# The prompt's up-projection by seven products of half blocks, with the weight sums on POOL

## The chip, the cores and the metric

One NeuronCore of a Trainium2 chip runs the whole kernel; one launch, all inputs and outputs in HBM. The metric is the time of that core on the device in microseconds. Engines: PE (TensorE, with PEld for its weight loads), DVE (VectorE), ACT (ScalarE), POOL (GpSimd) and SP, which issues most of the DMAs.

## The reference, cut to what matters

An encoder layer is run on two sequences, "prompt" (512 tokens) and "sample" (1024 tokens), with the same weights in float32. After a mixer the layer has a channel sub-layer, and its first product is the widest of the layer: 1024 channels to 2 x 2816.

```python
D_MODEL, D_FF, CONV_F_WIDTH = 1024, 2816, 3
h = rms_norm(x, g_pre_ffn) * (1.0 + sc2) + sh2
up = depthwise_conv(h @ w_up, ffn_conv_w, ffn_conv_b, CONV_F_LEFT)   # 3 taps along the tokens
val, gate = up[..., :D_FF], up[..., D_FF:]
f = (jax.nn.gelu(gate) * val) @ w_down
x = x + gt2 * rms_norm(f, g_post_ffn)
```

`mod = silu(c) @ w_ada + b_ada` gives the scales, shifts and gates (`sc2`, `sh2`, `gt2`) for each sequence.

## The kernel before

Activations stand channel-major: 128 channels on the partitions, tokens along the free axis. Every float32 operand of a product is split into a high part (a rounded copy, on ACT, type fp32r) and a low part (the rest, a subtraction on DVE); a product is three passes, high x high, high x low and low x high, added up in PSUM. Each matmul brings its own weight load of 128x128.

The program is a flat list of `Step`s. A step has matmuls (`mm`), what follows them (`post`, evictions and elementwise work), and often a `Unit`, a block of 128 x 1024 weights: `load_unit` brings it by a DMA of SP into one of three `raw` buffers, `prep_unit` splits it into one of four `hl` buffers. `emit` (L192) writes the steps in order; ahead of step i it prepares the weights of the steps up to i + 3 (`AHEAD`) and has the loads go three units ahead (`RAW_BUFS`); `defer(fn, d)` puts a piece of work d steps later. There is no other scheduler: each engine runs its instructions in the order in which this loop wrote them, waits for the semaphores of others, and lets nothing overtake.

The prompt's up-projection is `up_steps` (L1391). It makes 22 pairs of column tiles (gate, then value), 44 steps of 8 channel blocks x 3 passes = 24 matmuls, each 128 weights wide with all 512 tokens moving. `conv_f` (L1371) evicts a tile from PSUM: ACT scales the centre tap, DVE adds the two others (`scalar_tensor_tensor`, 128x511). The gate goes through gelu on ACT, DVE multiplies, and the result `fo` stays in SBUF for the down-projection. Into this list `weave` puts the 24 side steps of `ada_steps(5)` and `gate_steps`: 16 dot products of 128x1024 on DVE (L360) that form the gate `gt2`, four small DVE instructions on them (the last two write `gtg`), a PE transpose of `gtg` (`gate_rows`, L390), and a DMA round trip; one side step stands ahead of each product step from the third on.

Before it run the sample's output projection, after it the prompt's down-projection (`rows_steps`), and later the sample's up-projection `up_quads` (L1213). That one already makes two column tiles (20 pairs of 22) by seven products of blocks rather than eight: halves of the 1024 channels and halves of the 1024 tokens, so that a product moves 512 tokens; all block sums there are done by DVE, the parts of a product are split 512 columns at a time (`part`, L1289 and L1290).

Of the kernel before, what the change touches and what calls it, by code (L numbers as in the profile page):

```python
# [45 lines left out]
V_FW = 168  # L46
V_FB = 300
# [4 lines left out]
class Seq:  # L52
    def __init__(self, name, idx, n, x, y):
        self.name, self.idx, self.n, self.x, self.y = name, idx, n, x, y
        self.nf = 1024 // n
        self.tt = n // 128
        self.chunks = n // 512
        self.groups = KT // self.nf
        self.pq_tiles = self.tt // 2
# [7 lines left out]


class Step:
    def __init__(self, mm=None, post=None, unit=None, pre=None, loads=()):  # L70
        self.mm, self.post, self.unit, self.pre, self.loads = mm, post, unit, pre, loads


class Enc:
# [104 lines left out]
    def prep_to(self, k):  # L179
        while self.pp < min(len(self.units), k):  # L180
            self.load_to(self.pp + 1)
            u = self.units[self.pp]
            if u.unit is not None and (u.unit.parts or u.unit.dma) and self.pp + 2 > k:
                break
            if u.pre is not None:
                u.pre()
            if u.unit is not None and u.unit.whole:
                self.prep_unit(u.unit)
            self.pp += 1
            self.load_to(self.pp + RAW_BUFS)  # L190

    def emit(self):  # L192
        pos = 0
        for i, s in enumerate(self.steps):
            while self.rl < min(len(self.steps), i + LOAD_AHEAD + 1):
                for f in self.steps[self.rl].loads:
                    f()
                self.rl += 1
            self.load_to(self.pp + RAW_BUFS)
            self.prep_to(pos + AHEAD + 1)  # L200
            if s.unit is not None or s.pre is not None:
                pos += 1
            if s.mm is not None:
                s.mm()
            if s.post is not None:
                s.post()
            due = [f for t, f in self.late if t <= self.now]
            self.late = [(t, f) for t, f in self.late if t > self.now]
            for f in due:
                f()  # L210
            self.now += 1
# [960 lines left out]
    def quad_sums(self, hb):  # L1172
# [37 lines left out]
            steps += [Step(post=both), Step(post=parts(("t1", "t2", "t3", "t4")))]  # L1210
        return steps

    def up_quads(self, sq, hb, dst, plain):  # L1213

        nc = self.nc
        steps = []
        table = self.a["w_up"]
# [32 lines left out]
        for g in range(plain):  # L1250
            box = {}
# [20 lines left out]
            for m, post in ((FT + g, post_g), (g, post_v)):  # L1272
                u = Unit(table[m], KT * 128, on_act=True)
                steps.append(Step(mm=lambda u=u, mm_all=mm_all: mm_all(u, 0), unit=u, post=post))

        ring = {"n": 0}
        quads = []
        for g in range(plain, FT):
            ua, ub = (Unit(table[m], KT * 128, whole=False) for m in (FT + g, g))
            b, w = {}, {}  # L1280
# [52 lines left out]
            def post(i, b=b, g=g):  # L1333
                def f():
# [21 lines left out]
            plan = [((0, 0), "p", 0), ("t2", "p", 1), ("t1", "q", 0), ("t3", "q", 1), ((1, 0), "p", 0), ((1, 1), "q", 0),  # L1356
                    ("t4", "q", 1)]
# [30 lines left out]
                    in1=acc[:, f, o], op0=ALU.mult, op1=ALU.add)  # L1388
        return acc

    def up_steps(self, sq, hb, fo):  # L1391
        nc = self.nc
        steps = []
        xh, xl = (lambda: hb["hi"]), (lambda: hb["lo"])
        for g in range(FT // sq.nf):
            box = {}

            def post_g(ps, g=g, box=box):
                acc = self.conv_f(sq, ps, FT + g * sq.nf)
                nc.scalar.activation(out=acc, in_=acc, func=AF.Gelu_apprx_tanh)  # L1400
                box["g"] = acc

            def post_v(ps, g=g, box=box):
                acc = self.conv_f(sq, ps, g * sq.nf)
                nc.vector.tensor_tensor(out=acc, in0=acc, in1=box.pop("g"), op=ALU.mult)
                fo[g] = acc
            steps += self.fm_steps(sq, self.a["w_up"], range(FT + g * sq.nf, FT + (g + 1) * sq.nf), xh, xl, post_g,
                                   on_act=True)
            steps += self.fm_steps(sq, self.a["w_up"], range(g * sq.nf, (g + 1) * sq.nf), xh, xl, post_v,
                                   on_act=True)  # L1410
        steps[-1].post, last = None, steps[-1].post

        def done():
            last()
            hb.clear()
        steps[-1].post = done
        return steps


def weave(main, side, at, stride):  # L1420
    out = []
    side = list(side)
    for i, s in enumerate(main):
        if i >= at and (i - at) % stride == 0 and side:
            out.append(side.pop(0))
        out.append(s)
    return out + side


# [12 lines left out]
@with_exitstack
def encoder(ctx: ExitStack, tc: tile.TileContext, a, outs):
    nc = tc.nc
    e = Enc(ctx, tc, a, outs)
    p, s = e.p, e.s
    x2 = {q.name: e.dram([q.n, D], "x2" + q.name) for q in (p, s)}
    sig = {q.name: {(w, g): e.dram([128, 1024], f"sg{q.name}{w}{g}") for w in range(2) for g in range(q.groups)}
           for q in (p, s)}
    with tc.manual_schedule():  # L1450
        e.setup()
        h1 = {"p": {}, "s": {}}
        h2 = {"p": {}, "s": {}}
        hs = {q: {} for q in "ps"}
        yb = {q: {} for q in "ps"}
        pq = {q: {} for q in "ps"}
        z = {q: {} for q in "ps"}
        mg = {q: {} for q in "ps"}
        gate = {(q, i): {} for q in "ps" for i in range(2)}
        fo = {q: {} for q in "ps"}  # L1460

        def mix(q, heads):
            at = 4
            out = heads[:at] + e.pq_steps(q, pq[q.name], heads[:at]) + heads[at:]
            out += e.ya_steps(q, h1[q.name], hs[q.name], yb[q.name])
# [12 lines left out]
        _, heads = e.mix_heads(s, h1["s"], hs["s"], sig["s"])
        steps += place(mix(s, heads), e.ada_steps(3) + e.ada_steps(2, (1,)) + e.ada_steps(4),
                       [0, *range(8, 37), *range(36, 46), *range(40, 48)])  # L1480
        pa, pbt = e.h_steps(p, x2["p"], 1, h2["p"])
        steps += weave(e.merge_steps(s, yb["s"], z["s"], sig["s"], mg["s"]),
                       e.gate_steps(s, 0, gate["s", 0]) + pa, 8, 1)
        steps += weave(e.rows_steps(s, a["w_o"], mg["s"], gate["s", 0], a["x_sample"], x2["s"]), pbt, 4, 2)

        steps += weave(e.up_steps(p, h2["p"], fo["p"]),
                       e.ada_steps(5) + [Step()] * 2 + e.gate_steps(p, 1, gate["p", 1]), 2, 1)
        sa, sbt = e.h_steps(s, x2["s"], 1, h2["s"], quads=True)
        steps += weave(e.rows_steps(p, a["w_down"], fo["p"], gate["p", 1], x2["p"], outs[0]),
                       sa + sbt, 0, 1)  # L1490
        fs = e.dram([FT, 128, 1024], "fs")
        steps += place(e.up_quads(s, h2["s"], fs, 2), e.quad_sums(h2["s"]), [0, 0, 1, 1, 2, 2, 3, 3])
        steps += weave(e.rows_steps(s, a["w_down"], fo["s"], gate["s", 1], x2["s"], outs[1], last=True, fsrc=fs),
                       e.gate_steps(s, 1, gate["s", 1]), 4, 1)

        e.begin(steps)
        e.lead_in(p, a["x_prompt"], first, h1["p"], (2, 2, 2, 2))
        e.emit()
        e.flush()
# [118 lines left out]
```

## Time and profile before

| | us |
|---|---|
| median of 3 runs (lowest, highest) | 2091.42 (2090.84, 2091.93) |
| the profiled execution, its own time | 2091.33 |
| its span, first to last instruction | 2089.6 |
| PE busy, of the span | 2063.0 |
| DVE busy | 1411.0 |
| ACT busy | 948.0 |
| POOL busy | 69.9 |

The span leaves 1.7 us around it. A matmul's row shows a duration that overlaps with the next one's, so what a matmul costs is read from the distance between starts, not from its duration. The same holds to a lesser degree for DVE: a row lasts a little longer than the distance to the next start.

### The profile page before, as it was taken

How to read it: one execution, taken by the hardware profiler on the slowest of the kernel's cores; microseconds unless marked ns; L12 is line 12 of the kernel's file. 1: busy time of each engine (PE TensorE's matmuls, PEld its weight loads, DVE VectorE, ACT ScalarE, POOL GpSimd, SP SyncE). 2: the span in 40 equal slices, each digit the busy share in tenths (PEclk: the TensorE clock that was granted, in tenths of full speed). 3: DMA queues.
4: the chain of work that ended last, by engine and by line, in shares of the span. 5: the costliest groups of instructions: out<-in, count | busy, mean ns of one | idle time of the engine just before them, and what ended most of it. 6: DMA issues, size and time to landing. Idle time of an engine off the chain costs nothing.

```text
span 2089.6 us, 24382 instructions
## 1 busy us (share of the span) xinstructions
PE 2063.0 (99%) x9591; PEld 1685.7 (81%) x9591; DVE 1411.0 (68%) x1805; ACT 948.0 (45%) x1224; POOL 69.9 (3%) x154
## 2 busy tenths in 40 slices
PE   7999999999999999999999999999999999999998
PEld 6877788888888888888888888887888888888886
DVE  5667788667677556666576555759788888875543
ACT  2387555264654722145333336533444444444442
POOL 0100010100000000000100001000000000000000
PEclk9999999999999999999999999999999999999999
DMA  9933666643333325434543324232122222384322
GB/s 338 315 120 135 221 240 202 211 141 107 100 116 107 106 88 210 166 101 162 193 150 111 98 104 171 91 115 78 70 85 77 81 91 71 105 317 172 132 98 104
DMA packets 94451, 297.76 MB, mean 143 GB/s; under 512 B 9312, under 2 KB 20992, under 8 KB 93824
## 3 DMA queue, kind: packets, MB, share of 16 engines
q1 hardware_dynamic: 87968, 278.24, 37.9%
q0 software_dynamic: 5216, 13.74, 2.2%
q10 hardware_dynamic: 1152, 4.23, 0.5%
q8 instruction: 75, 1.23, 0.2%
q14 instruction: 40, 0.33, 0.0%
HBM read 248.93 MB, written 47.24 MB: 142 GB/s over the span
## 4 chain that ended last, share of the span: by engine, by line
PE 89%; DVE 5%; ACT 3%; issue 2%; DMA 1%; POOL 0%; DVEq 0%; POOLq 0%; SPq 0%; ACTq 0%
PE ps L223 88%; PE ps L226 1%; ACT th L733 1%; ACT th L723 1%; ACT ea L731 1%; DVE cf L1386 0%; DVE hx L113 0%; DVE hq L1184 0%; DVE th L754 0%; DVE th L759 0%; DVE th L757 0%; DVE hl L113 0%; ACT hl L110 0%; ACT xn L450 0%; ACT th L735 0%
## 5 line engine op out<-in xcount | busy, mean ns | idle before, releaser
L223 PE MATMUL ps<-hh,hl 128*128 128x512 f32 x2144 | 632.5, 394 | 3.7 <-DVE hl L113 2.9
L223 PEld LDWEIGHTS ps<-hh,hl 128*128 128x128 f32 x2144 | 402.2, 188 | 99.8 <-DVE hl L113 4.1
L223 PE MATMUL ps<-hl,ah 128*128 128x512 f32 x1440 | 452.8, 395 | 0.0
L113 DVE TENSOR_TENSOR hl<-raw,hl 128x1024 fp32r<-128x1024 f32 x224 | 268.5, 1202 | 187.1 <-ACT hl L110 186.6
L223 PE MATMUL ps<-hx,wq 128*128 128x512 f32 x1680 | 392.0, 395 | 2.3 <-ACT wq L1289 2.3
L223 PE MATMUL ps<-hl,hl 128*128 128x512 f32 x1072 | 380.1, 393 | 0.0
L223 PEld LDWEIGHTS ps<-hx,wq 128*128 128x128 f32 x1680 | 316.5, 188 | 77.6 <-ACT wq L1289 2.7
L110 ACT ACTIVATE hl<-raw 128x1024 fp32r<-128x1024 f32 x224 | 230.9, 1037 | 278.3 <-PE ps L223 242.2
L223 PEld LDWEIGHTS ps<-hl,ah 128*128 128x128 f32 x1440 | 269.0, 188 | 61.7
L223 PE MATMUL ps<-hl,al 128*128 128x512 f32 x720 | 283.9, 394 | 0.0
L223 PEld LDWEIGHTS ps<-hl,hl 128*128 128x128 f32 x1072 | 201.3, 188 | 47.0
L223 PEld LDWEIGHTS ps<-hl,al 128*128 128x128 f32 x720 | 135.3, 188 | 32.1
L1386 DVE SCALAR_TENSOR_TENSOR cf<-ps,vec,cf 128x511 f32<-128x511 f32 (+1 forms) x96 | 70.1, 788 | 73.5 <-ACT cf L1378 73.3
L223 PE MATMUL ps<-yh,hl 128*128 128x512 f32 x384 | 111.9, 394 | 0.3 <-DVE hl L113 0.3
L1289 ACT ACTIVATE wq<-wsum 128x512 fp32r<-128x512 f32 x80 | 48.5, 628 | 124.0 <-DVE wsum L1300 124.0
L1234 DVE SCALAR_TENSOR_TENSOR cf<-cq,vec,cf 128x1023 f32<-128x1023 f32 x80 | 102.1, 1277 | 0.0
L223 PEld LDWEIGHTS ps<-yh,hl 128*128 128x128 f32 x384 | 71.5, 188 | 16.7 <-DVE hl L113 0.7
L113 DVE TENSOR_TENSOR al<-fq,ah 128x512 fp32r<-128x512 f32 x88 | 57.2, 686 | 33.1 <-PE ps L223 18.4
L1378 ACT ACTIVATE cf<-ps,vec 128x512 f32<-128x512 f32 (+1 forms) x48 | 36.6, 809 | 91.5 <-PE ps L223 91.5
L776 ACT ACTIVATE sg<-ps 128x1024 f32<-128x1024 f32 x24 | 24.6, 1026 | 93.0 <-PE ps L223 92.9
L223 PE MATMUL ps<-yl,hl 128*128 128x512 f32 x192 | 65.2, 394 | 0.0
L1127 DVE TENSOR_TENSOR ro<-ps,gate 128x512 f32<-128x512 f32 x48 | 31.1, 686 | 48.7 <-ACT junk L1119 48.7
(187 smaller groups left out, 2367.2 us busy)
## 6 DMA issues: line engine op xcount, KB each, us to landing
raw<-in_w_up_dram SPq DMA_DIRECT2D x88, 512.0 KB, 3.5
raw<-in_w_down_dram SPq DMA_DIRECT2D x66, 512.0 KB, 3.6
ada<-in_w_adaT_dram SPq DMA_DIRECT2D x40, 512.0 KB, 5.0
raw<-in_w_o_dram SPq DMA_DIRECT2D x24, 512.0 KB, 3.5
fs<-cf SPq DMA_DIRECT2D x22, 512.0 KB, 2.6
fq<-fs SPq DMA_DIRECT2D x22, 512.0 KB, 6.3
hl<-wxb POOLq DMA_DIRECT2D x16, 516.0 KB, 5.3
ada<-in_w_ada_dram SPq DMA_DIRECT2D x16, 512.0 KB, 9.0
```

The lines of the kernel that those rows point to most:

```text
L110: nc.scalar.activation(out=hi, in_=src, func=AF.Copy)
L113: nc.vector.tensor_tensor(out=lo, in0=src[:, 0:keep], in1=hi[:, 0:keep].bitcast(F32), op=ALU.subtract)
L223: self.nc.tensor.matmul(*args, **kw)
L226: self.nc.tensor.transpose(*args)
L723: nc.scalar.activation(out=t[:, f, :], in_=ps[:, f, :], func=AF.Tanh, scale=0.5, bias=self.halfb[:, b:b + 1])
L731: nc.scalar.activation(out=ea[:, f, :], in_=r[:, f, :], func=AF.Exp, scale=self.nk4[:, k:k + 1], bias=self.nk4[:, k:k + 1])
L776: self.nc.scalar.activation(out=t, in_=ps, func=AF.Tanh, scale=0.5)
L1127: nc.vector.tensor_tensor(out=rows[o][:, cols], in0=p, in1=gate["gate"][:, cols], op=ALU.mult)
L1234: nc.vector.scalar_tensor_tensor(out=box[key][:, o], in0=c[:, i], scalar=self.vec[:, V_FW + 3 * m + t:V_FW + 3 * m + t + 1], in1=box[key][ ...
L1289: nc.scalar.activation(out=hi, in_=src, func=AF.Copy)
L1378: nc.scalar.activation(out=acc[:, f, :], in_=ps[:, f, :], func=AF.Identity, scale=w[:, 1:2], bias=self.vec[:, V_FB + m:V_FB + m + 1])
L1386: nc.vector.scalar_tensor_tensor(out=acc[:, f, o], in0=ps[:, f, o.start + d:o.stop + d], scalar=w[:, tap:tap + 1], in1=acc[:, f, o], op0=A ...
```

## The change

`up_steps` goes away. `up_halves` does the prompt's first two pairs of tiles as before (`plain`, 4 steps of 24 matmuls of 512 tokens) and the other 20 pairs by seven products of blocks: weights in halves of 512 channels (a1, a2 of the gate tile `ua`, and of the value tile `ub`), activations in halves of 512 channels by 256 tokens. A product has 4 channel blocks x 3 passes = 12 matmuls that move 256 tokens. `half_sums` forms the four sums of activation blocks once (t1 to t4) and splits them. The four sums of weight blocks of each pair (s1 to s4, 128x512) are done by POOL, as are the low part of one of the seven weight blocks and the product of value and gelu. `Step` gets its own `ahead` (5 in place of 3) and `look`. The side steps stand at every ninth place from the 44th step on, and those that find no place follow the last product.

```diff
 class Step:
+    def __init__(self, mm=None, post=None, unit=None, pre=None, loads=(), ahead=None, look=None):
+        self.ahead, self.look = ahead or AHEAD, look or RAW_BUFS
...
+    def up_halves(self, sq, hb, fo, plain):
...
+            def part(i, src, eng, w=w):
...
+                nc.scalar.activation(out=hi, in_=src, func=AF.Copy)
+                self.defer(lambda: eng.tensor_tensor(out=lo, in0=src, in1=hi.bitcast(F32), op=ALU.subtract), 1)
...
+                    if i in (0, 1):
+                        part(i, ua.raw[:, (a1, a2)[i]], nc.vector)
+                    if i == 2:
+                        s12, s34 = (self.big([128, 2, 512], name="wsum") for _ in range(2))
+                        b["s"] = s1, s2, s3, s4 = s12[:, 0, :], s12[:, 1, :], s34[:, 0, :], s34[:, 1, :]
+                        nc.gpsimd.tensor_tensor(out=s1, in0=ub.raw[:, a1], in1=ub.raw[:, a2], op=ALU.add)
+                        nc.gpsimd.tensor_tensor(out=s2, in0=s1, in1=ua.raw[:, a1], op=ALU.subtract)
+                        nc.gpsimd.tensor_tensor(out=s3, in0=ua.raw[:, a1], in1=ub.raw[:, a1], op=ALU.subtract)
+                        nc.gpsimd.tensor_tensor(out=s4, in0=ua.raw[:, a2], in1=s2, op=ALU.subtract)
+                    if i in (2, 3, 4):
+                        part(i, b["s"][(1, 0, 2)[i - 2]], nc.vector)
+                    if i == 5:
+                        part(i, ub.raw[:, a2], nc.vector)
+                    if i == 6:
+                        part(i, b.pop("s")[3], nc.gpsimd)
...
+                    for j in range(KT // 2):
+                        for q, (l, r) in enumerate(((hi, 0), (hi, 1), (lo, 0))):
+                            self.mmul(
+                                b[ps][:, half, 0:256], lhsT=l[:, j * 128:(j + 1) * 128], rhs=block(x, j, r),
...
+                    if i in (0, 2, 4):
...
+                        copy(b["v"][i // 2], b["p"][:, 0, 0:256])
...
+                        out = lambda: nc.gpsimd.tensor_tensor(out=room(g), in0=fb, in1=fa, op=ALU.mult)
+                        for fn, d in ((cb, 1), (ca, 1), (tb, 2), (sb, 3), (ta, 3), (sa, 4), (gelu, 5), (out, 6)):
+                            self.defer(fn, d)
...
+            plan = [((0, 0), "p", 0), ((1, 0), "q", 1), ("t2", "p", 0), ("t1", "q", 0), ("t3", "p", 0), ("t4", "p", 0),
+                    ((1, 1), "q", 0)]
...
+            steps += q[1:5] + [m[0] for m in quads[i + 1:i + 2]] + q[5:]
...
-        steps += weave(e.up_steps(p, h2["p"], fo["p"]),
-                       e.ada_steps(5) + [Step()] * 2 + e.gate_steps(p, 1, gate["p", 1]), 2, 1)
+        up = place(e.up_halves(p, h2["p"], fo["p"], 2), e.half_sums(h2["p"]), [0, 0, 0, 0, 1, 1, 1, 1])
+        steps += place(up, e.ada_steps(5) + [Step()] * 2 + e.gate_steps(p, 1, gate["p", 1]), range(44, 250, 9))
```

POOL, from the end of the sample's output projection on. Before, its queue goes there from that stage's row scales (`sm`, 128x1) straight to those of the next norm:

```order
L1132 TENSOR_TENSOR sm_7929<-sm_7764,mhalf 128x1
L1132 TENSOR_TENSOR sm_7931<-sm_7769,mhalf 128x1
L1132 TENSOR_TENSOR sm_7933<-sm_7776,mhalf 128x1
L1132 TENSOR_TENSOR sm_7935<-sm_7781,mhalf 128x1
L467 TENSOR_SCALAR sm_9502<-sm_9498 128x1
L468 TENSOR_TENSOR sm_9499<-sm_9502,mhalf 128x1
```

After, 20 such groups stand between the two, one for each pair of tiles (`wsum`: sums of weight blocks, `wq`: a low part, `fo`: the product of an earlier pair):

```order
L1331 TENSOR_TENSOR wsum_8734<-raw_8577,raw_8619 128x512
L1332 TENSOR_TENSOR wsum_8734<-raw_8577,wsum_8733 128x512
L1382 TENSOR_TENSOR fo_8655<-cf_8672 128x512
L1318 TENSOR_TENSOR wq_8827<-wsum_8734,wq_8827 128x512
L1329 TENSOR_TENSOR wsum_8862<-raw_8757 128x512
L1330 TENSOR_TENSOR wsum_8862<-wsum_8862,raw_8712 128x512
```

Six instructions of 128x512, all with both inputs in SBUF, moved or were added to POOL for each pair.

PE around the transpose of `gtg`. Before, it stands amid the up-projection, between two steps of it:

```order
L223 MATMUL ps_8662<-hh_7692,hl_8586 128x512 x2
L223 MATMUL ps_8662<-hl_7693,hl_8586 128x512
L223 MATMUL ps_8662<-hh_7692,hl_8586 128x512
L226 MATMUL ps_8729<-ident,gtg 16x128
L223 MATMUL ps_8735<-hh_7398,hl_8620 128x512
L223 MATMUL ps_8735<-hl_7399,hl_8620 128x512
```

After, it stands between the last product of the up-projection and the first of the down-projection (`ah`, `al`: the split `fo`):

```order
L224 MATMUL ps_10682<-hh_7692,wq_10662 128x256 x2
L224 MATMUL ps_10682<-hl_7693,wq_10662 128x256
L224 MATMUL ps_10682<-hh_7692,wq_10662 128x256
L227 MATMUL ps_10837<-ident,gtg 16x128
L224 MATMUL ps_10860<-hl_10739,ah_10735 128x512 x2
L224 MATMUL ps_10860<-hl_10739,al_10736 128x512
```

The transpose moved from the middle of the stage to its end.

DVE, from the add that waits for the last product of the up-projection (`cq`) to the write of `gtg`. Before, the write of `gtg` follows a weight split in mid-stage:

```order
L113 TENSOR_TENSOR hl_8586<-raw_8481,hl_8586 128x1024
L370 TENSOR_TENSOR mod<-mod,vec 128x8 x2
L379 TENSOR_TENSOR gtg<-mod,vec 128x8 x2
L113 TENSOR_TENSOR hl_8620<-raw_8519,hl_8620 128x1024
L1386 SCALAR_TENSOR_TENSOR cf_8649<-ps_8595,vec,cf_8649 128x511
```

After:

```order
L1359 TENSOR_TENSOR cq_10695<-ps_10682,vq_10641 128x256
L114 TENSOR_TENSOR al_10809<-fo_8907,ah_10808 128x1024
L114 TENSOR_TENSOR hl_10812<-raw_10742,hl_10812 128x1024
L361 SCALAR_TENSOR_TENSOR adap_10817,mod<-ada_10700,cs_1513 128x1024
L361 SCALAR_TENSOR_TENSOR ada_10700,mod<-ada_10700,cs_1516 128x1024
L1270 SCALAR_TENSOR_TENSOR cf_10805<-cq_10695,vec,cf_10805 128x511
L361 SCALAR_TENSOR_TENSOR adap_10823,mod<-ada_10733,cs_1513 128x1024
L1270 SCALAR_TENSOR_TENSOR cf_10805<-cq_10695,vec,cf_10805 128x511
```

Behind these follow two more taps, a fourth dot product, the two adds on `mod` and the two on `gtg`: fifteen DVE instructions from that add to the write for which PE's transpose waits.

## Rows read from the trace of the kernel before

**Rows 1.** The page, part 1: busy time of each engine, whole span.

```profile
PE 2063.0 (99%) x9591; PEld 1685.7 (81%) x9591; DVE 1411.0 (68%) x1805; ACT 948.0 (45%) x1224; POOL 69.9 (3%) x154
```

**Rows 2.** The chain that ended last, in order of time: start, us, what.

```profile
991.11 155.71 PE ps L223 x672
...
1146.92 166.99 PE ps L223 x720
```

**Rows 3.** Busy time by engine in the prompt's up-projection (span, busy, instructions, clock).

```profile
core 0: us, PE busy (x) PEld busy (x) DVE busy (x) ACT busy (x) POOL busy (x), PEclk, DMA share, GB/s
1024.20:1269.10 244.90, 244.90 (x1058) 198.27 (x1057) 150.33 (x186) 89.56 (x106) 4.45 (x8) 1.00 0.35 122
```

**Rows 4.** Timeline, PE, first matmuls of this stage and of the next (start, us).

```profile
1024.24 0.40 PE L223 MATMUL ps<-hh,hl 128*128 128x512 f32 x1
...
1269.12 0.62 PE L223 MATMUL ps<-hl,ah 128*128 128x512 f32 x2
```

**Rows 5.** Timeline, PE, the mixer's products with 258 columns.

```profile
276.99 1.63 PE L223 MATMUL ps<-z,hl 128*128 128x258 f32 x12
278.45 0.29 PE L223 MATMUL ps<-ze,hl 96*128 96x258 f32 x1
...
280.15 1.61 PE L223 MATMUL ps<-z,hl 128*128 128x258 f32 x12
281.60 0.28 PE L223 MATMUL ps<-ze,hl 96*128 96x258 f32 x1
```

**Rows 6.** Groups by line and shape, DVE (count, busy us, mean ns, idle before).

```profile
L1290 DVE TENSOR_TENSOR wq<-wsum,wq 128x512 fp32r<-128x512 f32 x80 | 54.6, 683 | 1.4 <-ACT wq L1289 1.4
L360 DVE SCALAR_TENSOR_TENSOR adap<-ada,cs 128x1024 f32<-128x1024 f32 x24 | 29.2, 1218 | 0.0
L439 DVE TENSOR_TENSOR wxf<-ps,wxf 128x252 fp32r<-128x252 f32 x16 | 5.9, 409 | 0.0
L113 DVE TENSOR_TENSOR hl<-raw,hl 128x1024 fp32r<-128x1024 f32 x216 | 263.1, 1221 | 174.6 <-ACT hl L110 174.1
```

**Rows 7.** Timeline, DVE, back to back: distances between starts.

```profile
1170.69 2.72 DVE L1386 SCALAR_TENSOR_TENSOR cf<-ps,vec,cf 128x511 f32<-128x511 f32 x4 [4.74 <-ACT cf L1378]
...
1643.59 0.69 DVE L1290 TENSOR_TENSOR wq<-wsum,wq 128x512 fp32r<-128x512 f32 x1
1644.19 0.69 DVE L1300 TENSOR_TENSOR wsum<-raw,raw 128x512 f32<-128x512 f32 x1
```

**Rows 8.** Timeline, POOL, in the mixer's merge.

```profile
280.10 1.14 POOL L467 TENSOR_SCALAR sm<-sm 128x1 f32<-128x1 f32 x1 [7.87 <-ACT xn L450]
281.33 0.55 POOL L468 TENSOR_TENSOR sm<-sm,mhalf 128x1 f32<-128x1 f32 x1
...
289.33 0.19 POOL L467 TENSOR_SCALAR sm<-sm 128x1 f32<-128x1 f32 x1 [2.31 <-ACT xn L450]
...
298.55 0.80 POOL L467 TENSOR_SCALAR sm<-sm 128x1 f32<-128x1 f32 x1 [5.03 <-ACT xn L450]
```

**Rows 9.** Timeline, DVE, at the same places.

```profile
279.97 1.23 DVE L113 TENSOR_TENSOR hl<-raw,hl 128x1024 fp32r<-128x1024 f32 x1
281.11 0.69 DVE L1028 TENSOR_TENSOR yb<-ps,vs 128x516 f32<-128x516 f32 x1
...
298.08 1.23 DVE L1011 TENSOR_TENSOR mg<-mg,yb 128x1024 f32<-128x1024 f32 x1
```

**Rows 10.** Groups by line and shape, ACT.

```profile
L110 ACT ACTIVATE hl<-raw 128x1024 fp32r<-128x1024 f32 x216 | 226.1, 1053 | 278.3 <-PE ps L223 242.2 <-issue 15.5 <-DMA raw<-in_w_ga_dram 6.0
L1289 ACT ACTIVATE wq<-wsum 128x512 fp32r<-128x512 f32 x80 | 48.5, 628 | 124.0 <-DVE wsum L1300 124.0
L432 ACT ACTIVATE wxf<-ps 128x252 fp32r<-128x252 f32 x16 | 4.9, 398 | 0.6 <-PE ps L223 0.6
```

**Rows 11.** Timeline, PE, and clock (second row, as Rows 3) after the lead-in's idle 1.88 us.

```profile
27.10 0.47 PE L223 MATMUL ps<-hh,lwh 128*128 128x512 f32 x1 [1.88 <-DVE hh L112]
...
27.00:33.00 6.00, 5.56 (x21) 3.40 (x25) 5.83 (x12) 0.16 (x1) 0.00 (x0) 0.72 1.09 370
```

More of the change, by code (lines that the diff above doesn't have):

```diff
@@ L69 @@
 class Step:
-    def __init__(self, mm=None, post=None, unit=None, pre=None, loads=()):
+    def __init__(self, mm=None, post=None, unit=None, pre=None, loads=(), ahead=None, look=None):
         self.mm, self.post, self.unit, self.pre, self.loads = mm, post, unit, pre, loads
+        self.ahead, self.look = ahead or AHEAD, look or RAW_BUFS
 class Enc:
@@ L189, in prep_to @@
             self.pp += 1
-            self.load_to(self.pp + RAW_BUFS)
+            self.load_to(self.pp + u.look)
     def emit(self):
@@ L199, in emit @@
             self.load_to(self.pp + RAW_BUFS)
-            self.prep_to(pos + AHEAD + 1)
+            self.prep_to(pos + s.ahead + 1)
             if s.unit is not None or s.pre is not None:
@@ L1211, in quad_sums, with half_sums, join, f @@
         return steps
+    def half_sums(self, hb):
+        nc = self.nc
+        steps = []
+        for j in range(2):
+            box = {}
+            def join(r, j=j, box=box):
+                def f():
+                    box[r] = self.big([128, 2, 512], name="hq")
+                    for i in range(2):
+                        k = 4 * r + 2 * j + i
+                        nc.vector.tensor_tensor(
+                            out=box[r][:, i, :], in0=hb["hi"][k].bitcast(F32), in1=hb["lo"][k].bitcast(F32), op=ALU.add)
+                return f
+            def sums(box=box):
+                b11, b12 = (box[0][:, :, c * 256:(c + 1) * 256] for c in range(2))
+                b21, b22 = (box[1][:, :, c * 256:(c + 1) * 256] for c in range(2))
+                ta, tb = (self.big([128, 2, 2, 256], name="tq") for _ in range(2))
+                box["t1"], box["t2"], box["t3"], box["t4"] = ta[:, 0], ta[:, 1], tb[:, 0], tb[:, 1]
+                nc.vector.tensor_tensor(out=box["t1"], in0=b12, in1=b11, op=ALU.subtract)
+                nc.vector.tensor_tensor(out=box["t2"], in0=b22, in1=box["t1"], op=ALU.subtract)
+                nc.vector.tensor_tensor(out=box["t3"], in0=b22, in1=b12, op=ALU.subtract)
+                nc.vector.tensor_tensor(out=box["t4"], in0=b21, in1=box["t2"], op=ALU.subtract)
+            def parts(box=box):
+                for key in ("t2", "t1", "t3", "t4"):
+                    x = self.big([128, 2, 2, 256], F32R, name="hx")
+                    self.split(x[:, 0], x[:, 1], box[key], act=True)
+                    hb.setdefault(key, []).append(x)
+                box.clear()
+            steps += [Step(post=join(0)), Step(post=join(1)), Step(post=sums), Step(post=parts)]
+        return steps
@@ L1389, in conv_f @@
         return acc
[L1391 to L1417, printed above, removed]
 def weave(main, side, at, stride):
```

105 lines of the change are left out of this document (added).

## The prediction

> **What bounds the kernel now.** I read the page's busy times first, then the chain that ended last, then the stage that the change touches, then single rows of the timeline. PE is busy for 2063.0 of the span's 2089.6 us [rows 1], and the chain passes through the prompt's up-projection in two unbroken pieces of PE alone, apart from the one transpose of `gtg` [rows 2]. [...] So it lasts as long as its matmuls: from 1024.24 to 1269.12, 244.9 us [rows 4], for 44 x 24 = 1056 of them, 0.232 us each. The reader is to see that PE waits for nobody here, and that the others have room only because a pair of tiles gives them 48 x 0.232 = 11.1 us.
>
> **PE's part.** A 256-column matmul is not in the stage, but the mixer has 258-column ones with a weight load each: twelve start-to-start in 1.46 us and in 1.45 us [rows 5], so 0.121 us. That is more than half of 0.232, and I take it. A pair of tiles is then 7 x 12 x 0.121 = 10.2 us in place of 11.1. The stage's PE work: 4 plain steps, 96 x 0.232 = 22.3, and 20 x 10.2 = 203.3, together 225.6 us. The ceiling of the gain is 19.3 us; an eighth of the work goes on paper, but a matmul with half the columns costs 52% of a full one.
>
> **What DVE and POOL must do in these 10.2 us.** DVE, for each pair: six low parts of 128x512, 0.60 from start to start where they stand back to back, though a row lasts 0.68 [rows 6, 7]; four taps at 2.72 / 4 = 0.68 [rows 7]; 16 dot products over 20 pairs, 0.8 x 1.22 [rows 6]; three adds of 256 columns out of PSUM at 0.41 [rows 6]. The first three kinds read both inputs from SBUF: 3.60 + 2.72 + 0.98 = 7.3 us. The adds, 1.2 us, read one from PSUM. By itself DVE has 8.5 us of work and fits.
>
> POOL gets six instructions of 128x512 for each pair, and the trace has none such. From below I bound one by DVE's 0.60, since I see no reason for POOL to stream faster. From above by POOL's own two-input instruction of a single column, 0.55 undisturbed [rows 8], plus a stream at DVE's 0.68: 1.23. POOL's one-column scale takes only 0.19 [rows 8], so most of the 0.55 is the power that it computes; I take 1.05, nearer to the upper end. Six make 6.3 us, which alone also fits.
>
> They do not fit together, and that is the heart of it. At 280.10 POOL starts a scale of one column which takes 1.14 us and ends at 281.24; DVE's subtraction with both inputs in SBUF had begun at 279.97 and ended at 281.20. At 298.55 the same: POOL's 0.80 ends at 299.35, DVE's instruction, begun at 298.08, at 299.31 [rows 8, 9]. With no such DVE row beside it, at 289.33, POOL's scale takes 0.19. And at 281.33 POOL's next instruction keeps its 0.55 while DVE runs a subtraction with one input in PSUM (281.11 to 281.80) [rows 8, 9]. So an instruction of DVE with two SBUF inputs shuts POOL's read out until it ends, 0.04 us before POOL goes on. That the reverse holds, POOL shutting out DVE, the trace doesn't show; but whoever goes first, the two kinds can't stream at the same time, so a pair costs their sum: 7.3 + 6 x 1.05 + 6 x 0.04 = 13.8 us. The bounds for POOL's instruction give 7.3 + 3.6 = 10.9 and 7.3 + 7.4 + 0.2 = 14.9. All of these exceed PE's 10.2.
>
> [...]
>
> **ACT** has seven copies of 0.63, four evictions of 256 columns at 0.40 [rows 10], two centre taps and a gelu of about 0.8, 0.8 and 0.6: 8.2 us of 10.2. It fits, but its queue now holds copies that wait for POOL's sums ahead of evictions that PE waits for: the fifth and the sixth product of a pair go into the PSUM region of one that has just been evicted, with a single other product, 1.45 us, between. So late sums stop PE at once, and the six products of look-ahead don't hide a rate that is too low. A second loop: the low part on POOL waits for ACT behind the centre taps of the pair before, and the next pair's sums queue behind it. Even undisturbed I price that at 0.2 us a pair.
>
> **The start.** The 24 DVE instructions and 8 copies of `half_sums` lie beside the 22.3 us of plain steps. The low part for the second product stands behind the evictions of the last plain tile (two taps, one product: 0.77 + 1.36 + 0.69 + 0.60 = 3.4 us with ACT's centre tap), while the first product covers 1.45: I take 2.5 us with waits, from 0 to 4.
>
> **The end.** The side steps that find no place now follow the last product, and PE's transpose of `gtg` stands ahead of the down-projection. It waits for DVE's queue: after the last product an add 0.4, two low parts of 1024 columns 2.4 [rows 6], four dot products 4.9, four taps 2.7, four small ones about 0.6: 11.0 us. DVE in turn waits for ACT's 1024-column copies at 1.05 [rows 10], up to 5 us. I take 13 us of idle PE, from 11 to 16; before, the transpose lay in mid-stage and cost nothing. [...]
>
> **The sum**, against the profiled execution's own 2091.33 us (0.09 below the median): out 244.9; in 22.3 + 20 x 13.8 + 2.5 + 13 + 2 = 315.8 us. That is +70.9, so 2162 us. Nothing after the stage has slack to give it back, since PE is the chain there too. What of the runs lies within 0.2%, 4.2 us, a measurement can't tell from no change.
>
> **The rivals.**
> 1. *POOL reads beside DVE*, or its instructions are so short that PE stays the bound. One mechanism, in the 20 pairs; it decides at the pair's period for which the stage breaks even: (244.9 - 22.3 - 17.5) / 20 = 10.26 us. At 10.2 the gain of 19.3 meets 17.5 of start and end: 2090; with the loop's 0.2 us, 2094; with a short end (5 us) 2082. Against it speak the two rows of a POOL instruction stretched to DVE's end. For it: these were one-column instructions, and nothing shows a long one.
> [...]
> [...]
>
> That the seven products wouldn't be what runs is no rival: the order shows them.
>
> **How the numbers follow.** Forecast, 12.8 to 15 us a pair (2142 to 2186): 0.56. Rival 1: 0.17, of it faster by over 0.2% (below 2087) 0.08, within 0.2% 0.08, slower 0.01. Rival 2: 0.16. Rival 3: 0.11. The predicted time is the forecast's, 2162. Rivals 2 and 1 below 2106 are left out, and of rival 3 what lies above 2210: 2106 to 2210 holds the forecast, rival 2 and most of rival 3's lower half, 8 times in 10. Faster 0.08, same 0.08, slower 0.84.
>
> **What would show it.** In the profile after: PE's starts 0.121 us apart within a product, and gaps between products that end on ACT, DVE or POOL; 13 to 15 us from one pair's first product to the next; POOL rows of 128x512 that last well over 1.05 us where DVE's two-input rows run beside them, and DVE low parts (0.68 now) stretched where POOL came first; the adds out of PSUM at their 0.41. A PE gap of over 10 us that ends on DVE `gtg`, ahead of the first matmul with `ah`. I am wrong if POOL rows stay near 1 us beside undisturbed DVE rows and a pair takes 10.2 to 10.5 us; or if the 256-column matmul is not 0.121; or, at the right total, if the gaps end on evictions or weight DMAs rather than on the two engines' sum.

## The result and the profile after

The changed kernel takes 2183.16 us (median of four runs, 2180.14 to 2184.40) against 2091.22 before (2090.84 to 2091.93): 1.0441 times as long, 95% interval 1.0428 to 1.0454, some 92 us slower. The forecast was 2162 us, the range 2106 to 2210. So the direction and the range held, and the forecast itself was 21 us too low.

The profiled execution has a span of 2180.8 us. First the busy times of the page of the changed kernel, and the head of its chain that ended last by line, to be held against [rows 1, 2]:

```profile
PE 2073.5 (95%) x10311; PEld 1725.9 (79%) x10311; DVE 1578.0 (72%) x1960; ACT 1014.9 (47%) x1423; POOL 264.3 (12%) x274
...
PE 75%; DVE 16%; ACT 4%; issue 3%; POOL 1%; DMA 1%; DVEq 0%; POOLq 0%; SPq 0%; ACTq 0%
PE ps L224 74%; DVE cf L1270 5%; DVE wq L1318 3%; PE ps L227 1%; DVE cq L1359 1%; DVE hx L114 1%; ACT th L734 1%; ACT th L724 1%; ACT ea L732 1%; DVE ro L1139 1%; DVE hl L114 1%; DVE ada L361 0%; DVE adap L361 0%; DVE cf L1577 0%; DVE hq L1185 0%
```

PE is not the whole chain any more: DVE has 16% of it, with the convolution's taps (L1270) and the low parts of the weight blocks (L1318) at its head. The next fence is the table of busy times by stretch: the stage (answers [rows 3]), then its steady part, its end, and the first 6 us of the down-projection. Columns: stretch, its length, busy us and instructions of each engine, granted clock, share and GB/s of DMA.

```profile
core 0: us, PE busy (x) PEld busy (x) DVE busy (x) ACT busy (x) POOL busy (x), PEclk, DMA share, GB/s
1024.60:1358.90 334.30, 252.77 (x1772) 236.69 (x1771) 321.18 (x346) 157.00 (x304) 200.20 (x125) 0.90 0.28 93
1084.00:1321.00 237.00, 188.11 (x1362) 178.44 (x1361) 230.41 (x235) 115.01 (x231) 156.33 (x98) 0.92 0.27 87
1344.20:1358.90 14.70, 0.43 (x2) 0.43 (x3) 14.19 (x23) 5.29 (x8) 4.33 (x2) 0.64 0.57 195
1358.90:1365.00 6.10, 6.10 (x21) 4.82 (x21) 1.50 (x2) 3.03 (x4) 1.98 (x3) 0.75 0.66 218
```

The stage runs from 1022.88 (first `hh,hl` on PE) to 1358.51 (first `hl,ah`): 335.6 us where it took 244.9 [rows 4]. In its steady part DVE is occupied for 230.41 of 237 us, POOL for 156.33, PE for 188.11. An instruction of DVE or POOL counts as busy while it is stopped (in e1, below, DVE's twelve subtractions, 7.30 us alone, have rows of 19.04 us beside POOL's), so these shares say who is in the way, not how much work there is. The groups by line between 1040 and 1380 us show that (count, busy us, mean ns, idle before):

```profile
L1270 DVE SCALAR_TENSOR_TENSOR cf<-cq,vec,cf 128x511 f32<-128x511 f32 x80 | 118.0, 1494 | 0.2
L1318 DVE TENSOR_TENSOR wq<-raw,wq 128x512 fp32r<-128x512 f32 x60 | 68.4, 1142 | 0.0
L1318 DVE TENSOR_TENSOR wq<-wsum,wq 128x512 fp32r<-128x512 f32 x60 | 58.1, 991 | 0.0
L1359 DVE TENSOR_TENSOR cq<-ps,vq 128x256 f32<-128x256 f32 x60 | 24.7, 413 | 10.2 <-PE ps L224 8.5 <-ACT vq L1356 1.3
L1331 POOL TENSOR_TENSOR wsum<-raw,raw 128x512 f32<-128x512 f32 x19 | 32.9, 1730 | 0.0
L1318 POOL TENSOR_TENSOR wq<-wsum,wq 128x512 fp32r<-128x512 f32 x20 | 29.0, 1450 | 86.0 <-ACT wq L1317 86.0
```

The taps, 0.68 us from start to start before [rows 7], are on record with a mean of 1.49; the low parts, 0.683 before [rows 6], with 1.14 and 0.99; the adds that read one input from PSUM have 0.413, like the subtraction of 252 columns that they were priced by (0.409 [rows 6]). Where the two engines meet, the timeline of POOL and then of DVE (start, us) looks like this:

```profile
1164.67 1.73 POOL L1331 TENSOR_TENSOR wsum<-raw,raw 128x512 f32<-128x512 f32 x1
1166.36 1.73 POOL L1332 TENSOR_TENSOR wsum<-raw,wsum 128x512 f32<-128x512 f32 x1
...
1165.18 1.77 DVE L1318 TENSOR_TENSOR wq<-raw,wq 128x512 fp32r<-128x512 f32 x1
1166.87 1.76 DVE L1270 SCALAR_TENSOR_TENSOR cf<-cq,vec,cf 128x511 f32<-128x511 f32 x1
```

Each engine starts one instruction every 1.69 us, and DVE's row ends some 0.55 us behind POOL's. With DVE's 0.60 in it, POOL's share of a turn is 1.09 us.

What PE waits for, from 1020 to 1400 (engine and tile, releaser, us in total, times, longest):

```profile
PE ps L224 <- DVE cq L1359: 31.6, 22, 4.0
PE ps L224 <- ACT vq L1356: 20.9, 13, 2.7
PE ps L227 <- DVE gtg L380: 14.6, 1, 14.6
PE ps L224 <- DVE wq L1318: 9.1, 5, 6.1
PE ps L224 <- DVE cf L1270: 4.0, 1, 4.0
```

The end of the stage in PE's timeline, with its idle time in brackets:

```profile
1358.47 0.38 PE L227 MATMUL ps<-ident,gtg 128*16 128x128 f32 x1 [14.56 <-DVE gtg L380]
```

The waits inside the pairs end on evictions (`cq`, `vq`). The adds into `cq` are not slow themselves (0.413); they stand late in DVE's queue. That ACT's copies into `vq` are late for the same reason is shown only by the run without the sums (e4, below). I take the time of a pair from the gelus on ACT, one in each pair by blocks: 1083.0 to 1358.2 for 19 intervals, 14.48 us. With that the 92 us are

- 22.3 + 20 x 14.48 - 244.9 = 67.0 us in the pairs,
- 14.6 us for `gtg` and some 1.7 us behind it, in which eight matmuls take 3.53 us (1358.51 to 1362.04) in place of 8 x 0.232,
- what is left, 8.6 us, put down to the start of the stage.

### The profile page after: what moved, and what is told of

It reads as the page before. It is cut to its first block, busy times and chain, and to the rows that moved or that the text cites. A ratio compares the mean times of both kernels' runs of the same rounds, so it can differ in the third digit from the quotient of the medians.

```text
span 2180.8 us, 26374 instructions
## 1 busy us (share of the span) xinstructions
PE 2073.5 (95%) x10311; PEld 1725.9 (79%) x10311; DVE 1578.0 (72%) x1960; ACT 1014.9 (47%) x1423; POOL 264.3 (12%) x274
## 4 chain that ended last, share of the span: by engine, by line
PE 75%; DVE 16%; ACT 4%; issue 3%; POOL 1%; DMA 1%; DVEq 0%; POOLq 0%; SPq 0%; ACTq 0%
PE ps L224 74%; DVE cf L1270 5%; DVE wq L1318 3%; PE ps L227 1%; DVE cq L1359 1%; DVE hx L114 1%; ACT th L734 1%; ACT th L724 1%; ACT ea L732 1%; DVE ro L1139 1%; DVE hl L114 1%; DVE ada L361 0%; DVE adap L361 0%; DVE cf L1577 0%; DVE hq L1185 0%
## 5 line engine op out<-in xcount | busy, mean ns | idle before, releaser
L224 PE MATMUL ps<-hx,wq 128*128 128x512 f32 (+1 forms) x2640 | 525.5, 359 | 37.6 <-ACT vq L1356 20.9
L224 PEld LDWEIGHTS ps<-hx,wq 128*128 128x128 f32 x2640 | 440.7, 192 | 119.8 <-ACT vq L1356 24.1
L224 PE MATMUL ps<-hh,hl 128*128 128x512 f32 x1504 | 431.8, 394 | 3.2 <-DVE hl L114 2.6
L114 DVE TENSOR_TENSOR hl<-raw,hl 128x1024 fp32r<-128x1024 f32 (+1 forms) x184 | 220.0, 1198 | 172.2 <-ACT hl L111 171.9
L224 PEld LDWEIGHTS ps<-hh,hl 128*128 128x128 f32 x1504 | 282.1, 188 | 71.1 <-DVE hl L114 3.9
L111 ACT ACTIVATE hl<-raw 128x1024 fp32r<-128x1024 f32 (+1 forms) x184 | 190.0, 1035 | 249.1 <-PE ps L224 207.3
L224 PE MATMUL ps<-hl,hl 128*128 128x512 f32 x752 | 254.5, 394 | 0.0
L224 PE MATMUL ps<-hh,wq 128*128 128x256 f32 x480 | 105.4, 308 | 31.6 <-DVE cq L1359 19.2
L1270 DVE SCALAR_TENSOR_TENSOR cf<-cq,vec,cf 128x511 f32<-128x511 f32 x80 | 118.0, 1494 | 0.2
L224 PEld LDWEIGHTS ps<-hh,wq 128*128 128x128 f32 x480 | 85.2, 210 | 37.4 <-DVE cq L1359 22.5
```

What stands on the lines that cost most here:

```text
L111: nc.scalar.activation(out=hi, in_=src, func=AF.Copy)
L114: nc.vector.tensor_tensor(out=lo, in0=src[:, 0:keep], in1=hi[:, 0:keep].bitcast(F32), op=ALU.subtract)
L224: self.nc.tensor.matmul(*args, **kw)
L1270: return lambda: nc.vector.scalar_tensor_tensor(out=out[:, o], in0=c[:, i], scalar=w[:, t:t + 1], in1=out[:, o], op0=ALU.mult, op1=ALU.add)
```

## The experiments

The theory: an instruction of POOL that reads SBUF and one of DVE with two SBUF inputs take turns, and the sum of the turns is a pair's time; start and end are costs of their own. The main rival: the loops between ACT's copies, POOL's sums, the low parts and PE set the time, and the long rows are only waits.

**The turns by themselves (e1).** A kernel of its own, run once, twelve instructions of each kind back to back:

```
dve_two : vector.tensor_tensor(out, tok, y, subtract)     pool_two: gpsimd.tensor_tensor(out, tok, y, subtract)
dve_one : vector.tensor_tensor(out, PSUM, tok, subtract)  pool_one: gpsimd.tensor_scalar(out, tok, 0.5, mult)
dve_tap : vector.scalar_tensor_tensor, 511 columns        pool_none: gpsimd.memset(out)
```

> The whole layer is left out; the kernel only runs twelve instructions of a kind one behind the other, alone and in pairs, all of 128x512 float32. Theory (an instruction of POOL that reads SBUF and one of DVE that reads two SBUF inputs take turns): DVE's subtraction alone 0.60 us from start to start, POOL's alone 1.1 to 1.3, both together about 1.7 for each of the two engines, so that twelve of each last some 20 us; the same for DVE's convolution tap beside POOL (1.7 to 1.8), and for POOL's one-input multiplication. With one of DVE's inputs in PSUM, with a POOL memset that reads nothing, or with ACT beside POOL, each engine keeps the pace it has alone. Rival (the two read side by side, and what stretched the rows in the changed kernel were waits for buffers and weights): both together finish twelve of each in the time of the slower alone, 13 to 16 us. [...]

Its timeline (start, us for the twelve): POOL, then DVE.

```profile
15.74 15.00 POOL L53 TENSOR_TENSOR go<-tok,y 128x512 f32<-128x512 f32 x12 [15.30 <-DVE ao L70]
31.52 20.04 POOL L53 TENSOR_TENSOR go<-tok,y 128x512 f32<-128x512 f32 x12 [0.78 <-DVE ao L70]
52.41 14.71 POOL L53 TENSOR_TENSOR go<-tok,y 128x512 f32<-128x512 f32 x12 [0.86 <-DVE ao L70]
67.98 20.10 POOL L53 TENSOR_TENSOR go<-tok,y 128x512 f32<-128x512 f32 x12 [0.85 <-DVE ao L70]
88.97 18.71 POOL L56 TENSOR_SCALAR go<-tok 128x512 f32<-128x512 f32 x12 [0.89 <-DVE ao L70]
107.94 5.65 POOL L59 MEMSET go<- 128x512 f32 x12 [0.27 <-DVE go L70]
...
7.68 7.30 DVE L43 TENSOR_TENSOR vo<-tok,y 128x512 f32<-128x512 f32 x12
31.41 19.04 DVE L43 TENSOR_TENSOR vo<-tok,y 128x512 f32<-128x512 f32 x12
52.38 7.26 DVE L46 TENSOR_TENSOR vo<-ps,tok 128x512 f32<-128x512 f32 x12
67.87 19.09 DVE L49 SCALAR_TENSOR_TENSOR vo<-tok,y 128x511 f32<-128x511 f32 x12
88.83 9.79 DVE L43 TENSOR_TENSOR vo<-tok,y 128x512 f32<-128x512 f32 x12
108.42 7.31 DVE L43 TENSOR_TENSOR vo<-tok,y 128x512 f32<-128x512 f32 x12
```

Alone DVE's twelve take 7.30 us (0.61 each) and POOL's 15.00 (1.25); side by side (31.5) they take 20.04, 1.67 for a turn of both, and so with the tap (68.0). Beside a DVE instruction with one input in PSUM (52.4) both keep their own pace, 7.26 and 14.71; beside a memset (108) DVE keeps its 7.31, and beside ACT both keep theirs (POOL's twelve 14.71 us, DVE's 7.31). Nothing here waits for a buffer or a weight, so the turns are shown. POOL's part of a turn is 1.67 - 0.61 = 1.06 us. Of the matmuls of 256 columns e1 has 72 in two groups of 36, with a weight load each: 8.9 us busy, 0.124 each with the overhang of the last of each 36; from start to start it is 0.12 (one of 512 columns and 36 of 256 behind it last 4.70 us, from 27.88). So the 0.121 of the prediction is their price by themselves, too.

**POOL's work given to DVE (e2).** Less work in parallel, on the engine that was already fuller.

```
-nc.gpsimd.tensor_tensor(out=s1, ...)      (s1 to s4, and fo)
+nc.vector.tensor_tensor(out=s1, ...)
-part(i, b.pop("s")[3], nc.gpsimd)
+part(i, b.pop("s")[3], nc.vector)
```

> POOL's six instructions of a pair of tiles (four sums of weight blocks, the low part of the seventh product, the product of the two tiles) are given to DVE; nothing else is changed. Theory (the two engines take turns, so a pair costs the sum of their instructions, POOL's at 1.09 us each): on DVE each of the six costs 0.60 instead, a pair 8.5 + 6 x 0.60 = 12.1 us in place of 14.5, and the kernel is 48 us shorter, near 2135 us; between 2125 and 2150. Rival (the loops of latency between ACT, POOL and PE, or the weight buffers, set the period): DVE, now with 12.1 us of its own work, gives no relief, 14 us a pair or more, 2170 to 2200 us. Rival (POOL does read beside DVE): the kernel becomes slower than the changed one, for DVE gets 3.6 us more of work a pair: over 2190.

Measured: 2143.02 us, ratio 1.0251 to before, interval 1.0236 to 1.0266, that is 40 us less than the changed kernel. The gelus run from 1080.2 to 1318.9, 12.56 us a pair. In the groups of this kernel the rows are back at their old length, and DVE is idle for 14.8 us ahead of its adds:

```profile
L1270 DVE SCALAR_TENSOR_TENSOR cf<-cq,vec,cf 128x511 f32<-128x511 f32 x80 | 57.9, 744 | 0.1
L1318 DVE TENSOR_TENSOR wq<-wsum,wq 128x512 fp32r<-128x512 f32 x80 | 53.8, 682 | 0.0
L1359 DVE TENSOR_TENSOR cq<-ps,vq 128x256 f32<-128x256 f32 x60 | 25.0, 419 | 14.8 <-PE ps L224 14.8
```

Theory and sign hold; the 8 us above 2135 go with a pair of 12.56 in place of 12.1 (20 x 0.46 = 9.2), and 14.8 us of idle DVE cover them.

**The sums not read (e4).** POOL's four sums of weight blocks are left out; POOL writes ones in their place.

```
-nc.gpsimd.tensor_tensor(out=s1, in0=ub.raw[:, a1], in1=ub.raw[:, a2], op=ALU.add)   (and s2 to s4)
+nc.gpsimd.memset(s1, 1.0)
```

> The four sums of weight blocks on POOL are left out: in their place POOL writes ones to the same tiles, by four instructions of the same size that read nothing. All waits, buffers, weight loads and copies stay. Theory (taking turns): two of POOL's six reads are left, and a pair needs 14.5 - 4 x 1.09 = 10.2 us by the turns, or PE's own 10.2; with some waits 10.3 to 11.3 us, so 64 to 84 us shorter than the changed kernel, 2099 to 2119 us. If POOL's writes held DVE up as its reads do, the pair would keep 12 us or more. Rival (loops of latency, buffers): the chain of waits is the same, each sum about half as long; 13 to 14.5 us a pair, 2150 to 2183 us.

Measured: 2105.22 us (one run); gelus from 1077.5 to 1280.7, 10.69 us a pair. With the same buffers and copies the loops need no more than that. A memset is shorter than a sum, too (0.47 us in e1, against 1.25), so the loops are shorter here by that much, and this run by itself doesn't exclude them; e9 takes them up from the other side. PE's waits on the evictions, 31.6 and 20.9 us in the changed kernel, are nearly gone:

```profile
PE ps L224 <- DVE cq L1359: 4.6, 7, 1.0
PE ps L224 <- ACT vq L1356: 1.0, 2, 0.5
```

From 1100 to 1260 of this kernel, columns as above:

```profile
1100.00:1260.00 160.00, 155.71 (x1294) 153.50 (x1293) 155.30 (x226) 108.87 (x215) 80.32 (x91) 1.00 0.38 124
```

PE is busy for 155.7 of 160 us, at a granted clock of 1.00, and nearly the bound again. This run is also the ceiling of the change as it stands: with sums that hold nobody up it would still be 15 us slower than before, since start and end cost more than the pairs gain.

**The end of the stage (e3).** The modulation's dot products are spread so that `gtg` is transposed within the stage.

```
-... e.gate_steps(p, 1, gate["p", 1]), range(44, 250, 9))
+... e.gate_steps(p, 1, gate["p", 1]), range(16, 250, 5))
```

> Only the places of the side steps are changed: the dot products of the modulation, and the transpose of gtg behind them, are spread from the 16th step of the stage on, every fifth step, in place of the 44th and every ninth, so that all of them find a place within the stage. Theory (the 14.6 us that PE waits for gtg at the stage's end, and the 2 us of low clock behind them, are a cost of their own): 14 to 17 us shorter, 2166 to 2169 us; four more dot products in the stage, each a DVE instruction with two SBUF inputs of 1.2 us, give back up to 5 of it: up to 2174. Rival (DVE's queue is behind by as much anyway, and the down-projection's first matmuls would wait for the last taps and products in place of gtg): less than 5 us, 2178 to 2184.

Measured: 2172.86 us, ratio 1.0395 (1.0377 to 1.0412), 10.3 us less than the changed kernel. PE's wait for `gtg` is gone; a pair takes 14.69 us (gelus 1089.5 to 1368.7), 0.21 more, 4 us in all. The four dot products that now lie in the stage, at 1.22 us each, would account for that. So the end is a cost of its own, of which DVE takes a part back.

Both edits together (e6):

> Both edits together: POOL's six instructions of a pair on DVE, and the side steps spread so that gtg is done in the stage. Theory (two costs, each by itself: the turns and the end): the second edit is worth here what it was worth in the changed kernel, 10.3 us, so 2143.0 - 10.3 = 2132.7, between 2129 and 2137 us. Rival (with DVE the fullest engine, its queue is late at the stage's end in any case): 2139 us or more.

Measured: 2138.30 us (2133.04 to 2140.83), ratio 1.0224 (1.0208 to 1.0240). That is 4.7 us less than without the second edit, where 10.3 were expected; the median lies between the theory's range and the rival's. The profile doesn't show why. It is that of the fastest of the four executions, and this one is 10.4 us shorter than the profiled one of e2 (2133.04 and 2143.47), as the theory has it: PE's products by blocks take 266.4 us from the first start to the last (1045.59 to 1312.02) in place of 258.9 (1046.07 to 1304.99), 7.5 more, and the 14.3 us from there to the down-projection are down to 0.1. Of the 10.4 us, 6.7 are the difference of the two, an estimated 1.7, as in the changed kernel, the slower matmuls behind the wait that is gone, and the rest lies outside the stage. What is taken out of the end does come back in part in the pairs. But the other three executions are 4 to 8 us longer than the profiled one, and whether the two costs add is not settled.

**Weights and look-ahead (e5, e9).** First, in e5, a fourth buffer for raw weights, with the second load of a pair sooner:

```
-RAW_BUFS = 3
+RAW_BUFS = 4
-look={1: 4, 3: 6}
+look={1: 8, 3: 6}
```

> The changed kernel with a fourth buffer for raw weight blocks, and the second block of each pair of tiles is loaded four steps sooner. Theory (POOL and DVE take turns and their sum is the period): the loads were in time but at the start; 13.8 of the 14.5 us of a pair are the two engines' turns, so at most 0.7 us x 20 and the start's few us can come free: 2168 to 2186 us, most likely within 5 of the changed kernel's 2183. Rival (late weight blocks hold POOL's sums up): a pair falls below 13 us, 2150 us or less.

Measured: 2180.35 us, ratio 1.0427 (1.0411 to 1.0442), not to be told from the changed kernel. Late weights are not the cause. Then, in e9, one more product of preparation:

```
-ahead=None if end else 5
+ahead=None if end else 6
```

> The changed kernel with the weight parts prepared six products ahead in place of five; nothing else. Theory (13.8 of the 14.5 us of a pair are the turns of POOL and DVE; the other 0.7 are stretches in which both wait for ACT's copies): the turns stay, at most 0.7 x 20 = 14 us come free: 2169 to 2186 us. Rival (latency from copy to low part to product sets the period): one more product of 1.45 us of slack takes most of the 4.3 us above PE's 10.2 away, below 2150 us.

Measured: 2174.75 us, ratio 1.0404 (1.0387 to 1.0421), 8.4 us less. The gelus run from 1085.6 to 1349.4: 13.88 us a pair. The waits of POOL for ACT's copies and gelus between 1080 and 1350, first in the changed kernel, then in this one:

```profile
POOL wq L1318 <- ACT wq L1317: 56.2, 18, 4.1
POOL fo L1382 <- ACT cf L1381: 33.9, 17, 5.3
```

```profile
POOL wq L1318 <- ACT wq L1317: 15.5, 14, 2.6
POOL fo L1382 <- ACT cf L1381: 60.3, 19, 7.8
```

So the look-ahead is worth 0.6 us of the 14.48, and POOL's wait for the copy ahead of its low part, with the next sums queued behind it, is mostly gone; 13.88 us stay, where the rival had most of the 4.3 us above PE's 10.2 come free. POOL isn't full in either kernel: in its place it now waits longer for the gelu ahead of `fo`, and its idle time falls only from 90.1 to 75.8 us. DVE is the full one: from 1100 to 1260 it is occupied (work and stops) for 155.94 of 160 us in the changed kernel and for 153.91 in this one. The same sum with e1's prices is 7.3 + 6 x 1.06 = 13.7.

**Fewer pairs by blocks (e7, e8, e10).** With both edits of above (the side steps now at every fourth place), six of the pairs go back to plain products, so that by the engines' totals PE is the bound again. First e7, the mixed kernel; then e8, with three plain pairs at the front; then e10, with the taps put later:

```
+MORE = (4, 7, 10, 13, 16, 19)     # these pairs plain, each behind two by blocks; RAW_BUFS = 4
+            if late[i] + 1 in MORE:
+                steps += direct[late[i] + 1]
```

> As the kernel with both edits, and of the 20 pairs of tiles six (the 4th and every third behind it, counted from 0) go back to plain products, one behind each two pairs by blocks; a fourth buffer for raw weights. So 8 plain pairs and 14 by blocks. Theory (rates of engines decide): PE has 8 x 11.13 + 14 x 10.2 = 231.9 us, DVE some 8 x 6.6 + 14 x 12.1 = 222.2 us, so PE is the bound again: 244.9 - 231.9 = 13 us gained, some 6 lost at the start and up to 8 by waits between products: 2084 to 2092 us. Rival (the latency from a product's last matmul to the eviction that frees its PSUM region costs PE in every pair by blocks, whatever the load of DVE): the 12.56 us that such a pair took with DVE doing all stay, 8 x 11.13 + 14 x 12.56 = 264.9, and with the start's 6 us 2117 us, between 2108 and 2122.

> As the mixed kernel, but with three plain pairs ahead of the first pair by blocks in place of two: 9 plain pairs and 13 by blocks. Theory: PE's work is 9 x 11.13 + 13 x 10.2 = 232.8 us, 0.9 more; the 11 us of cover for the sums over the tokens take away the 6 us that PE waits at the start, so 3 to 6 us less than the mixed kernel, 2079 to 2088 us. Rival (the start waits for the weights of the first pair by blocks, which are loaded and summed only ahead of it, however many plain pairs stand before): within 2 us of the mixed kernel.

> The mixed kernel, but in its six plain pairs within the stage the convolution taps, the gelu and the product are put one and two steps later, so that DVE's queue doesn't stand waiting for ACT's centre tap (26.7 us of idle DVE in the mixed kernel). Theory (DVE is full enough that its 26.7 us of idle ahead of the taps come back as PE's 39 us of waits): half to all of it, 2100 to 2114 us. Rival (PE's waits come from the evictions on ACT and DVE behind each product, not from DVE's total): within 5 us of the mixed kernel's 2127.

Measured: 2126.73 (ratio 1.0171, 1.0154 to 1.0188), 2127.82 (1.0176, 1.0161 to 1.0192) and 2126.68 us (1.0171, 1.0156 to 1.0186). The best of all versions that form their sums, and still 36 us behind the kernel before. The theories of all three missed (2084 to 2092, 2079 to 2088, 2100 to 2114); the rivals of e8 and e10, no gain over the mixed kernel, came true. The totals of the engines were the wrong guide here. PE's waits in e7, and then in e10:

```profile
PE ps L227 <- DVE cq L1364: 15.1, 13, 2.1
PE ps L227 <- ACT vq L1361: 12.9, 7, 3.1
PE ps L227 <- DVE wq L1323: 7.6, 2, 6.9
PE ps L227 <- DVE cf L1273: 3.4, 1, 3.4
```

```profile
PE ps L227 <- ACT vq L1373: 19.9, 8, 3.6
PE ps L227 <- DVE wq L1335: 13.4, 8, 7.2
PE ps L227 <- DVE cf L1273: 3.4, 1, 3.4
PE ps L227 <- DVE cq L1376: 3.0, 8, 0.4
```

39.0 us in the first, 39.7 in the second. They are not the whole loss: the stage lasts 284.2 us in e7 (1021.24 to 1305.41), 52.3 above PE's own 231.9, so 13.3 us are not waits. Part of them is PE's granted clock: 1.00 in the stage before, and in e7 0.80 from 1050 to 1080 and 0.96 to 0.98 from there to 1290. The later taps did take half of DVE's idle time behind ACT's centre taps away (28.4 us in the mixed kernel between 1030 and 1300, 12.5 here), but it came back as idle time ahead of the adds (14.4 to 30.2), and PE's waits moved from `cq` to `vq` and `wq`. So the time doesn't follow DVE's idle time behind the centre taps; all three lie even above the rival's 2117, and PE's waits end on taps, adds and copies that free a PSUM region and on low parts. Why these come late with DVE at about four fifths of its time isn't settled by these runs. Three plain pairs at the front in place of two gained nothing.

## Why the prediction held, and where its terms were off

**The heart held.** Turns of POOL and DVE, read off one-column scales in the mixer [rows 8, 9], are what makes most of the pair: e1 shows them in both directions (DVE's twelve 19.04 us in place of 7.30, POOL's 20.04 in place of 15.00), where the rows had shown only DVE first, and e2 the consequence, that giving POOL's work to the fuller engine is 40 us faster. Rival 1 is out by e1 and e4. Rival 2, in which an instruction of POOL costs a pair only 0.60 to 0.85 us, is out by e1: POOL's share of a turn is 1.06.

The rows of the changed kernel close the sum from DVE's side. Against its rows in e2, a tap lasts 0.75 us longer, a low part 0.46 or 0.31, a dot product some 0.34: 4 x 0.75 + 3 x 0.46 + 3 x 0.31 + 0.8 x 0.34 = 5.6 us in which a pair's DVE rows are stopped. With DVE's own 8.5 and 0.5 of idle time ahead of the adds that is 14.6, for a measured 14.48. The 5.6 are less than 6 x 1.06 = 6.4, so some of POOL's work ran beside the adds or the idle time; the prediction's sum puts all 1.2 us of the adds beside POOL.

By its letter one of the prediction's signs of being wrong came: PE's gaps end on evictions (`cq` 31.6 us, `vq` 20.9). That they are late because of the turns is shown by e4, where the evictions are the same and these waits fall to 4.6 and 1.0 us.

**POOL's instruction**, 1.05 from the bounds 0.60 and 1.23, measured 1.06 to 1.09 within a turn. Alone e1 has 1.25 from start to start, just above the upper bound.

**A pair** was forecast at 13.8 and took 14.48: 20 x 0.68 = 13.6 of the 21 us. The step that was mis-sized is the second loop, priced at 0.2 us and left out of the sum: 0.6 us go in e9 with one more product of look-ahead, and 13.88 are left. That these agree with the 13.8 so closely is in part luck: the sum puts all of the adds beside POOL, and counts no idle DVE.

**The start**, 2.5 us forecast with an upper bound of 4, took some 8.6, the largest miss for its size. I had put the 24 DVE instructions of `half_sums` beside the plain steps, as though DVE had room there. It hasn't, and the evictions of the plain tiles stand behind them in its queue. DVE, then PE:

```profile
1050.34 2.49 DVE L114 TENSOR_TENSOR hx<-tq,hx 128x512 fp32r<-128x512 f32 x4
1052.75 1.53 DVE L1270 SCALAR_TENSOR_TENSOR cf<-ps,vec,cf 128x511 f32<-128x511 f32 x2
...
1054.42 0.55 PE L224 MATMUL ps<-hh,wq 128*128 128x256 f32 x1 [3.97 <-DVE cf L1270]
1061.30 0.79 PE L224 MATMUL ps<-hh,wq 128*128 128x256 f32 x2 [6.11 <-DVE wq L1318]
```

PE waits 3.97 us for a plain tile's taps, and 6.11 for the low part of the first pair's second product, behind the taps of the last plain tile. The prediction had priced this second chain alone, at 3.4 us less 1.45 of cover.

**The end**: 13 us forecast, 14.56 measured. The sum's 2 us for the matmuls behind that wait were my estimate, and no run shows them: the first eight took 3.53 us, some 1.7 more than 8 x 0.232, at a granted clock of 0.75 (1358.90 to 1365.00). The four misses are 13.6 + 6.1 + 1.6 - 0.3 = 21.0 us; they add up by construction, as the start is what was left. **PE's price** of 0.121 held: within a product every third matmul starts 0.36 us after the last (1170.08, 1170.44, 1170.80).

**Rival 3**, a pair slower than the sum by the loops or by a lower granted clock of PE, was in part there. A product at 1183.80, behind waits of 2.66 and 0.87 us, has a granted clock of 0.58, and its matmuls start 0.21 us apart in place of 0.12:

```profile
1183.80:1188.70 4.90, 4.90 (x26) 4.90 (x27) 3.86 (x5) 4.88 (x10) 1.28 (x1) 0.58 0.64 210
```

The stage less PE's named waits (81.1 us in all, 0.9 of them for a copy of ACT) is 254.5 us, 28.9 more than the 225.6 of its work at 0.121 and 0.232. That part of it is the lower clock, the row above shows (0.58). That the pair was not longer by it, since DVE was full anyway, is argued and not shown: from 1100 to 1260 the granted clock was 0.92 in the changed kernel, 0.94 in e9 and 1.00 in e4, where only two of POOL's six instructions read.

## What to carry to other kernels

Before work is given to POOL, ask which DVE instructions read two inputs from SBUF in the same stretch: there, in e1, an instruction on POOL took 1.06 us from both engines where DVE did it in 0.61 itself. An algorithm with fewer multiplications is to be priced by what the smaller matmul measures (0.121 for half of 0.232, so 10.2 of 11.1 us a pair and not seven eighths), and its sums by the fullest queue, with the evictions that stand behind them. What is taken out of the end of a stage goes into somebody's queue in its middle; look whether that one is the bound. And engines with room in their totals can still keep PE waiting: in e7 DVE was busy for four fifths of the time, and PE waited 39 us.

## What the runs showed of the hardware that was not expected

POOL holds DVE up for less than its whole instruction. Two-input: 1.25 us alone, 1.06 in a turn. One-input multiplication: once DVE had finished, six took 8.75 us, 1.46 each, so it is slower than the two-input subtraction; beside it DVE ran twelve in 9.79 us, two for each of POOL's. DVE's own 7.3 us taken off, 2.5 us are left for the six of POOL's that ran in that time, 0.4 us of each. If each engine stopped the other for a whole instruction, one of each would take 1.46 + 0.61 = 2.07 us; POOL's scale with two DVE instructions beside it took some 1.66 (18.71 - 8.75 us for six). A memset, which writes only, did not hold DVE up: 7.31 us for its twelve beside it, 7.30 alone.
